# Seams of an MLP: buffers shared across stages, four operands by way of DRAM, another order of products in the down projection

## The chip, the cores and the metric

The kernel runs on one core of one Trainium2 chip. The metric is the device time of one execution in microseconds (us), the median of several runs. Profile times are counted from the start of the span that the profiler recorded.

## What is computed

One layer of a decoder trunk on 2048 rows of 1024 features: a norm, a token mixer (a delta rule group and a dilated attention group of heads), the output projection, and a gated MLP with a causal convolution over the sequence, then a last norm. The end of the layer is what this case is about:

```python
x = x + jnp.concatenate([y_a, y_b], axis=-1) @ w_out[l]
h = rmsnorm(x, ln2[l])
gate = causal_dwconv(h @ w_gate[l], ffn_conv[l])          # three taps, 2816 columns
x = x + (jax.nn.silu(gate) * (h @ w_up[l])) @ w_down[l]
return rmsnorm(x, ln_f)
```

All of it is float32. TensorE takes float32 in a rounded form, so each operand is split into a high and a low part (`split`, L65 to L68: a cast on ACT, then a subtraction on DVE), and each product is three matmuls (`mm3`, L71 to L75): high by high, high by low, low by high.

## The kernel before, in words

The MLP has three stages, each bound to the next by buffers.

**out_proj** (L978) goes through 16 tiles of 128 rows. For each it loads y from DRAM (`wr`, four blocks `yg` of the delta rule and four `ys` of the attention), casts it to yh and yl, and multiplies with w_out, whose eight blocks k are split into woh and wol (`w_out`, L860, two raw buffers `wor`; blocks 0 to 3 are made while the mixer still runs, 4 to 7 at the start of the MLP). The first three tiles (HEAD) run k=0 to 6 first, so that the last head's `ys` may come late. The residual is added on DVE, stored to x1, and normed (`norm2`), and the transposed result goes to DRAM in `hT`.

**gate_up** (L1027) uses Strassen's seven products: rows and features are halved, and for each of 11 pairs of column tiles (p), in each half of the rows (half), there are seven steps s, each of 24 matmuls 128x512 for gate and up (m=0 and 1). One p is 168 matmuls. A step needs one operand of the activations, `hc[s]` (four blocks k, high and low), which serves all 11 p of a half, and one of the weights, wh and wl, which is made two steps ahead (`prep`, AHEAD_W). Of the weights, s=0, 3 and 6 are plain blocks, the others sums made on POOL (sa, sb). `form(half, s)` makes `hc[s]`: s=0, 3, 5 from plain blocks of hT, s=1 and 4 by one subtraction on POOL, s=2 and 6 by one on POOL and one on DVE from an operand that is there already. For half 0 it runs in out_proj (s=0 to 2) and p=0, for half 1 in the last p of half 0 (p=10). `act` does the convolution, silu and product on DVE and ACT; `blocks` makes seven sums of the activation (five on POOL) and stores them in `act`.

**down_proj** (L1163) takes the seven products of the table DOWN, each for eight row groups q: one group is 33 matmuls, whose result is added to or subtracted from acc. Weights `w` are loaded one product ahead; for a sum of two weight blocks POOL adds them (L1183).

The order on each engine and queue is fixed when the program is built; every queue works in order. An instruction that waits holds all that is behind it. Transfers issued by SP also wait for a free slot of its queue.

Of the kernel before, what the change touches and what calls it, by code (L numbers as in the profile page):

```python
# [9 lines left out]
F32 = mybir.dt.float32  # L10
# [8 lines left out]
P = 128  # L19
# [858 lines left out]
def rms_scale(n, ss, src, junk):  # L878
# [12 lines left out]
DOWN = ((((0, 0), 1, (1, 1)), ((0, 0), 1, (1, 1)), ((0, 0, 1), (1, 1, 1))),  # L891
# [7 lines left out]
AHEAD_W = 2  # L899


def phase_e(n):

    with ExitStack() as ctx:
        n.wk = ctx.enter_context(n.pool("ewk"))
        n.lnb = n.wk.tile([P, D], F32, name="lnb")
        n.nc.sync.dma_start(n.lnb, n.a["ln2"].to_broadcast([P, D]))
        with ExitStack() as inner:
            mlp = Mlp(n, inner)
            mlp.out_proj()  # L910
            mlp.gate_up()
        down_proj(n)


class Mlp:
    def __init__(self, n, ctx):
        self.n, self.ctx = n, ctx
        nc = n.nc
        self.sm = ctx.enter_context(n.pool("esm"))
# [11 lines left out]
    def norm2(self, xt, t, tag=None):  # L931
# [3 lines left out]
        ss = n.wk.tile([P, 4], F32, tag="ss", name="ss", bufs=2)  # L935
        rms_scale(n, ss, xt, n.wk.tile([P, D], BF16, tag="junk", name="junk"))
        nc.vector.scalar_tensor_tensor(xt, xt, ss[:, 2:3], n.lnb, op0=ALU.mult, op1=ALU.mult)
# [34 lines left out]

    def out_proj(self):
        n, a = self.n, self.n.a
        nc, tc, v = n.nc, n.tc, n.nc.vector
        with ExitStack() as eo:
# [4 lines left out]
            wp = eo.enter_context(n.pool("ewp", 3))  # L981
            wo = n.wo
# [24 lines left out]
            first = (x for s in range(3) for x in self.form(0, s))  # L1007
            for t in range(HEAD):
                out_proj(t, range(7))
            for t in range(NT):  # L1010
# [5 lines left out]
                xt = xts[t] = n.wk.tile([P, D], F32, tag="xt", name="xt", bufs=3)  # L1016
# [5 lines left out]
                if t >= 11:  # L1022
                    for _ in range(3):
                        next(first, None)
# [3 lines left out]
    def gate_up(self):  # L1028
# [4 lines left out]
        self.hcp += [self.ctx.enter_context(n.pool("ehcb", 1, "right"))] * 4  # L1033
        op = self.ctx.enter_context(n.pool("ego", 1, "right"))
        steps = [(half, p, s) for half in range(2) for p in range(NP) for s in range(7)]
        raws, sums, made = {}, {}, {}

        def load(p, m, blocks):
            w = a["w_gate" if m == 0 else "w_up"]
            for i, j in blocks:  # L1040
                r = raws[m, i, j] = wp.tile([P, 512], F32, tag=f"r{m}{i}{j}", name=f"r{m}{i}{j}")
                nc.sync.dma_start(r, w[2 * p + i][:, 512 * j:512 * j + 512])

        def prep(i):

            half, p, s = steps[i]
            for m in range(2):
# [3 lines left out]
                new = lambda t: wp.tile([P, 512], F32, tag=f"{t}{m}", name=f"{t}{m}")  # L1051
# [65 lines left out]

        for i in range(AHEAD_W):
            prep(i)
# [266 lines left out]
```

## Time and profile before

| | us |
|---|---|
| median of 3 runs | 2922.37 (2922.06 to 2924.52) |
| the profiled execution, its own time | 2918.55 |
| its span | 2916.7 |
| TensorE busy in it | 2752.6 (94%) |
| DVE, ACT, POOL busy | 1669.9, 1131.9, 977.7 |
| mean granted TensorE clock | 0.964 |

Each number in the rows further down is of the one profiled execution. PE is the TensorE, PEld its weight loads, SPq the queue of SyncE that issues DMAs. `A <- B` after a wait names the instruction that ended it. PEclk of 1.00 is the engine's 2.4 GHz, 0.50 its 1.2 GHz. The MLP lies between 1300 and 2917; the mix ends at 1301, out_proj at about 1530, half 0 of gate_up at about 1980, half 1 at 2438.

### The profile page before, as it was taken

The numbers are of one execution on the slowest core, as the hardware profiler recorded it, in microseconds if no ns is written. First come the engines' busy times: TensorE is split into PE (matmuls) and PEld (weight loads), VectorE is DVE, ScalarE is ACT, GpSimd is POOL, SyncE is SP. The second block draws the span as 40 slices with busy tenths as digits, with TensorE's granted clock in tenths as the row PEclk, the third lists the DMA queues.
The fourth block names the chain that finished last, engine by engine and source line by source line (L and its number), as shares of the span: only waits on it lengthen the run. The fifth ranks groups of instructions, "written<-read, shape, count | busy, mean of one in ns | idle before, by whom it ended". The sixth has DMA issues, their size and how long they took to land.

```text
span 2916.7 us, 41147 instructions
## 1 busy us (share of the span) xinstructions
PE 2752.6 (94%) x14974; PEld 2332.3 (80%) x14974; DVE 1669.9 (57%) x2782; ACT 1131.9 (39%) x2349; POOL 977.7 (34%) x1191
## 2 busy tenths in 40 slices
PE   8999999899999999978998999996999996699999
PEld 8998777777899999966776888874888885588887
DVE  5205545725555555533347877778877776445554
ACT  5313554341165555552334333333333332222233
POOL 4200232131122232211116655656655554202231
PEclk9999999999799999988998999998999998899999
DMA  5222344465866665334654333344333325745553
GB/s 182 80 61 98 112 132 136 131 200 167 234 162 166 161 169 142 88 106 144 215 180 145 108 100 106 100 134 152 107 103 97 98 87 187 273 170 175 172 200 132
DMA packets 360665, 416.67 MB, mean 143 GB/s; under 512 B 83287, under 2 KB 249479, under 8 KB 360071
## 3 DMA queue, kind: packets, MB, share of 16 engines
q1 hardware_dynamic: 312848, 384.73, 42.8%
q10 hardware_dynamic: 45390, 20.90, 2.6%
q0 software_dynamic: 2224, 8.42, 1.0%
q8 instruction: 118, 1.93, 0.3%
q14 instruction: 85, 0.70, 0.1%
HBM read 282.16 MB, written 131.79 MB: 142 GB/s over the span
## 4 chain that ended last, share of the span: by engine, by line
PE 82%; DMA 6%; DVE 3%; issue 3%; POOL 3%; ACT 2%; SPq 1%; ACTq 0%; POOLq 0%; DVEq 0%
PE tp L75 7%; PE tp L74 6%; PE tp L73 6%; PE sc L75 6%; PE sc L74 6%; PE sc L73 6%; PE pv L75 5%; PE pv L73 5%; PE pv L74 5%; PE g L73 4%; PE g L75 4%; PE g L74 4%; PE pv L722 3%; PE sc L625 3%; PE sc L627 2%
## 5 line engine op out<-in xcount | busy, mean ns | idle before, releaser
L632 DVE CUSTOM_DVE_ANT_0 s<-sc,bias 128x256 f32<-128x256 f32 (+1 forms) x384 | 121.8, 363 | 130.3 <-PE sc L627 100.6
L1104 POOL TENSOR_TENSOR sm<-cv 128x512 f32<-128x512 f32 x110 | 178.4, 1653 | 52.8 <-issue 26.2
L1183 POOL TENSOR_TENSOR w<-w,w 128x512 f32<-128x512 f32 x55 | 89.1, 1642 | 269.1 <-DMA w<-in_w_down_dram 170.1
L67 ACT CAST ah<-ar 128x1408 fp32r<-128x1408 f32 x56 | 77.1, 1377 | 257.2 <-PE g L74 70.5
L722 PE MATMUL pv<-pt,sv 128*65 128x128 f32 x1200 | 168.0, 285 | 2.3 <-ACT pt L704 2.0
L625 PE MATMUL sc<-k,q 128*128 128x256 f32 (+1 forms) x384 | 156.4, 414 | 1.1 <-DVE m L632 1.0
L67 ACT CAST wh<-r 128x512 fp32r<-128x512 f32 x132 | 81.4, 619 | 192.7 <-issue 59.3
L694 ACT ACTIVATE s<-s,nm 128x256 f32<-128x256 f32 (+1 forms) x384 | 151.5, 460 | 11.7 <-POOL rb L769 6.6
L73 PE MATMUL g<-hch,wh 128*128 128x512 f32 x352 | 141.0, 401 | 14.4 <-DVE g L1143 9.8
L73 PE MATMUL sc<-hch,wh 128*128 128x512 f32 x352 | 140.7, 400 | 12.7 <-ACT hch L67 11.2
L722 PEld LDWEIGHTS pv<-pt,sv 128*65 128x65 f32 x1200 | 143.3, 145 | 5.5 <-ACT pt L704 4.8
L75 PE MATMUL sc<-hch,wl 128*128 128x512 f32 x352 | 140.5, 399 | 5.9 <-DVE wl L68 5.9
L75 PE MATMUL g<-hch,wl 128*128 128x512 f32 x352 | 140.5, 399 | 2.6 <-DVE wl L68 2.6
L68 DVE TENSOR_TENSOR wl<-r,wh 128x512 fp32r<-128x512 f32 x132 | 142.3, 1079 | 0.7 <-ACT wh L67 0.7
L627 PE MATMUL sc<-k,q 128*128 128x256 f32 (+1 forms) x384 | 142.7, 377 | 0.0
L704 ACT COPY pt<-tp 128x512 f32<-128x512 f32 (+1 forms) x152 | 87.7, 578 | 136.1 <-PE tp L701 129.2
L74 PE MATMUL sc<-hcl,wh 128*128 128x512 f32 x352 | 140.2, 398 | 0.0
L74 PE MATMUL g<-hcl,wh 128*128 128x512 f32 x352 | 139.8, 397 | 0.0
L73 PE MATMUL tp<-hch,wh 128*128 128x512 f32 x352 | 138.4, 393 | 0.0
L74 PE MATMUL tp<-hcl,wh 128*128 128x512 f32 x352 | 138.0, 392 | 0.0
L75 PE MATMUL tp<-hch,wl 128*128 128x512 f32 x352 | 138.0, 392 | 0.0
L1084 DVE SCALAR_TENSOR_TENSOR cv<-g,fcw,cv 128x1024 f32<-128x1024 f32 x88 | 132.7, 1508 | 0.8
(373 smaller groups left out, 8228.5 us busy)
## 6 DMA issues: line engine op xcount, KB each, us to landing
ar<-act SPq DMA_DIRECT2D x56, 704.0 KB, 4.2
w<-in_w_down_dram SPq DMA_DIRECT2D x132, 256.0 KB, 5.1
act<-sm SPq DMA_DIRECT2D x110, 256.0 KB, 2.3
r<-in_w_gate_dram SPq DMA_DIRECT2D x88, 256.0 KB, 2.7
r<-in_w_up_dram SPq DMA_DIRECT2D x88, 256.0 KB, 2.9
sm<-hT SPq DMA_DIRECT2D x72, 256.0 KB, 3.5
xt<-in_x_dram SPq DMA_DIRECT2D x32, 512.0 KB, 3.7
zn<-zn SPq DMA_DIRECT2D x32, 512.0 KB, 5.5
```

The costliest lines, as they stand in the source:

```text
L67: (first or nc.scalar.copy)(hi, src)
L68: (e or nc.vector).tensor_tensor(lo, src, hi.bitcast(F32), op=ALU.subtract)
L73: nc.tensor.matmul(ps, ah, bh, start=start, stop=False, skip_group_check=more)
L74: nc.tensor.matmul(ps, ah, bl, start=False, stop=False, skip_group_check=more)
L75: nc.tensor.matmul(ps, al, bh, start=False, stop=stop, skip_group_check=more)
L625: nc.tensor.matmul(r, self.cols(q2, d, u, False, full), self.cols(k1, d, u, prev, full), start=True, stop=False)
L627: nc.tensor.matmul(r, self.cols(q2, d, u, False, full), self.cols(k2, d, u, prev, full), start=False, stop=True)
L632: n.mark = v.tensor_tensor_reduce(out=s[:, r], in0=ps[:, r], in1=self.bias[d][:, bo:bo + r.stop - r.start], scale=1.0, scalar=-3e38, op0=A ...
L694: nc.scalar.activation(s, s, AF.Exp, bias=nm[:, col:col + 1])
L722: nc.tensor.matmul(dst, self.vcols(h, d, u, back), pt[:, j * P:(j + 1) * P], start=(back == int(prev)), stop=(back == 0))
L1084: v.scalar_tensor_tensor(cv, g[:, j:j + 1024], self.cw[:, x, j:j + 1], cv, op0=ALU.mult, op1=ALU.add)
L1104: gp.tensor_tensor(src, x(*op_[0]), x(*op_[2]), op=ALU.add if op_[1] > 0 else ALU.subtract)
```

## The change

Four things are done.

1. The three buffers of y (pool `ewp`) are opened at the very start of the MLP, on other space than before; gate_up then keeps its weights in them: wh and wl of both m lie in one tile of [128, 2, 512], and sa, sb and the raw block (0,1) in the three of `wr`. 
2. `form(0, 3)` moves into out_proj, which begins one tile earlier with this work; p=0 forms s=4, 5, 6 in its steps 0, 1, 2.
3. Of half 1, the operands s=1, 2, 4 and 6 are computed in p=1 to 6 of half 0 (`foresee`, one block at each odd step, 16 in all) and stored in DRAM (`hf`); in p=10 `recall` loads them, two DMAs of 1 MB each. `form(1, s)` is left for s=0, 3 and 5.
4. DOWN begins with a product of one weight block. acc is loaded one tile per group in the first 16 groups, and not all 16 tiles ahead of the second product. The pools of down_proj are opened in another order.

```diff
-DOWN = ((((0, 0), 1, (1, 1)), ((0, 0), 1, (1, 1)), ((0, 0, 1), (1, 1, 1))),
+DOWN = ((((0, 0), 1, (0, 1)), ((1, 1),), ((0, 0, -1), (0, 1, 1))),
+        (((0, 0), 1, (1, 1)), ((0, 0), 1, (1, 1)), ((0, 0, 1), (1, 1, 1))),
...
+EARLY = (1, 2, 4, 6)
...
 class Mlp:
     def __init__(self, n, ctx):
...
+        self.wp = ctx.enter_context(n.pool("ewp", 3))
+        self.wk = ctx.enter_context(n.pool("ewk"))
...
-        self.hcp = [ctx.enter_context(n.pool("ehca"))] * 3
+        self.hcp = [ctx.enter_context(n.pool("ehca"))] * 4
...
+    def foresee(self):
...
+        for k in range(4):
+            for s, first, rest in ((1, (1, 0), ((0, 0),)), (4, (1, 1), ((1, 0),)), (2, (0, 0), ((1, 1), (1, 0))),
+                                   (6, (0, 1), ((0, 0), (1, 1), (1, 0)))):
+                r = load(*first, k)
+                for x in rest:
+                    add = (s == 2 and x == (1, 1)) or (s == 6 and x == (1, 0))
+                    gp.tensor_tensor(r, r, load(*x, k), op=ALU.add if add else ALU.subtract)
+                self.keep(s, k, r)
+                yield
+
+    def keep(self, s, k, src):
+        n = self.n
+        t = self.wk.tile([P, 2, 512], F32R, tag="xt", name="hf", bufs=3)
+        split(n.nc, t[:, 0], t[:, 1], src)
+        n.nc.sync.dma_start(n.hf[s].rearrange("p (i k t) -> p i k t", i=2, k=4)[:, :, k], t.bitcast(F32))
+
+    def recall(self, s):
+        n = self.n
+        self.hc[s] = tuple(self.hcp[s].tile([P, 4, 512], F32R, tag=f"h{i}{s}", name=f"hc{i}{s}") for i in "hl")
+        for i in range(2):
+            t = self.hc[s][i].rearrange("p k t -> p (k t)").bitcast(F32)
+            n.nc.sync.dma_start(t, n.hf[s][:, 2048 * i:2048 * i + 2048])
...
-            wp = eo.enter_context(n.pool("ewp", 3))
-            wo = n.wo
+            wp, wo = self.wp, n.wo
...
-            first = (x for s in range(3) for x in self.form(0, s))
+            first = (x for s in range(4) for x in self.form(0, s))
...
-                if t >= 11:
+                if t >= 10:
...
+        three = [self.wp.tile([P, 2, 512], F32, tag="wr", name="wr") for _ in range(3)]
+        spare = dict(zip(("sa", "sb", "r01"), three))
...
+            lo = self.wp.tile([P, 2, 512], F32R, tag="gul", name="wl")
+            hi = self.wp.tile([P, 2, 512], F32R, tag="guh", name="wh")
...
-                if p == 0 and s < 4:
-                    for _ in self.form(0, s + 3):
+                if p == 0 and s < 3:
+                    for _ in self.form(0, s + 4):
                         pass
                 if p == NP - 1:
-                    for _ in self.form(1, s):
-                        pass
+                    if s in EARLY:
+                        self.recall(s)
+                    else:
+                        for _ in self.form(1, s):
+                            pass
+                elif p and s % 2 == 1:
+                    next(early, None)
...
         prep_a(1)
-        for t in (x for q in range(8) for x in (tile_of(q, 0), tile_of(q, 1))):
+        for t in (x for r in range(2) for q in range(8) for x in (tile_of(7 - q, r),)):
             acc[t] = cp.tile([P, D], F32, name=f"acc{t}")
-            nc.sync.dma_start(acc[t], n.x1[t])
...
+            if x < 16:
+                t = tile_of(q, x // 8)
+                nc.sync.dma_start(acc[t], n.x1[t])
```

How the order of the instructions moves is shown at three places. The first is SP's queue at the end of the mix: rb belongs to the attention, wor is raw w_out, lnb, fcw and xt (from x) are for the later stages, wr is y. Before:

```order
L762 DMA rb<-rden_130 64x512 x2
L907 DMA lnb<-in_ln_dram 128x1024
L924 DMA fcw<-in_fconv_t_dram 128x66
L1017 DMA xt<-in_x_dram 128x1024 x3
L872 DMA wor_12832<-in_w_out_dram 128x1024
L872 DMA wor_12833<-in_w_out_dram 128x1024
L995 DMA wr<-yg_170 128x4x128
L998 DMA wr<-ys_132 128x128
```

After, on the same queue:

```order
L762 DMA rb<-rden_130 64x512 x2
L1029 DMA wr<-yg_174 128x4x128
L1032 DMA wr<-ys_132 128x128
L1032 DMA wr<-ys_133 128x128
L1032 DMA wr<-ys_134 128x128
L1029 DMA wr<-yg_175 128x4x128
L919 DMA lnb<-in_ln_dram 128x1024
L925 DMA fcw<-in_fconv_t_dram 128x66
```

The loads of y have moved ahead of lnb, fcw, x and the last two wor, which now follow the y of all three head tiles.

The second place is p=3 of half 0. On POOL before, from the five sums of an activation (`sm<-cv`) to the weights of the next p (sa, sb; r are raw weights):

```order
L1104 TENSOR_TENSOR sm<-cv 128x512 x5
L1056 TENSOR_TENSOR sa_16139<-r_15986,r_16068 128x512
L1060 TENSOR_TENSOR sb_16184<-sa_16139,r_15984 128x512
L1087 COPY carry<-g_15886 128x2
L1056 TENSOR_TENSOR sa_16145<-r_15990,r_16070 128x512
```

On POOL after (sa and sb are now called wr):

```order
L1144 TENSOR_TENSOR sm<-cv 128x512 x5
L991 TENSOR_TENSOR sm<-sm 128x512 x6
L1127 COPY carry<-g_15877 128x2
L1098 TENSOR_TENSOR wr<-r_15983,r_16074 128x512
L1102 TENSOR_TENSOR wr<-wr,r_15981 128x512
L1098 TENSOR_TENSOR wr<-r_15987,r_16076 128x512
```

On SP after, in the same p, `act` is the store of a sum and r_16074 is the block r011 of the next p, which its sa needs:

```order
L1146 DMA act_0_170<-sm 128x4x128
L982 DMA sm<-hT_154 128x512
L982 DMA sm<-hT_155 128x512 x2
L1146 DMA act_0_172<-sm 128x4x128
L1082 DMA wr<-in_w_gate_dram 128x512
L1082 DMA wr<-in_w_up_dram 128x512
L982 DMA sm<-hT_154 128x512 x2
L999 DMA hf_157<-hf 256x1x512
L982 DMA sm<-hT_155 128x512 x3
L982 DMA sm<-hT_154 128x512
L999 DMA hf_159<-hf 256x1x512
L1082 DMA r_16074<-in_w_gate_dram 128x512
```

Six subtractions of `foresee` have come between the sums and sa on POOL; on SP their loads have come behind the act stores, and two stores of hf ahead of r011.

The third place is SP's queue between gate_up and down_proj. Before:

```order
L1196 DMA ar<-act_0_156 128x1408 x2
L1106 DMA act_1_165<-cv 128x4x128
L1106 DMA act_1_157<-sm 128x4x128
L1106 DMA act_1_161<-sm 128x4x128
L1106 DMA act_1_163<-sm 128x4x128
L1106 DMA act_1_167<-sm 128x4x128
L1106 DMA act_1_169<-sm 128x4x128
L1181 DMA w_21925<-in_w_down_dram 128x512
L1181 DMA w_21927<-in_w_down_dram 128x512
```

After:

```order
L1229 DMA w_21724<-in_w_down_dram 128x512
L1229 DMA w_21729<-in_w_down_dram 128x512
L1146 DMA act_1_165<-cv 128x4x128
L1244 DMA ar<-act_0_160 128x1408 x2
L1229 DMA w_21597<-in_w_down_dram 128x512
L1146 DMA act_1_169<-cv 128x4x128
L1146 DMA act_1_161<-sm 128x4x128
L1146 DMA act_1_163<-sm 128x4x128
```

Thirteen weight loads have moved ahead of the last p's act stores (two of them are shown), and the row of sixteen acc loads, which before followed the 22 weight loads, is spread over the groups.

## Rows read from the trace of the kernel before

**Rows 1.** Windows: us, then busy time (instructions) of each engine, PEclk, DMA share, GB/s.

```profile
1320.00:1360.00 40.00, 33.14 (x133) 26.25 (x134) 7.13 (x10) 5.86 (x9) 0.00 (x0) 0.86 0.33 94
1520.00:1600.00 80.00, 63.30 (x257) 49.88 (x256) 56.52 (x57) 32.75 (x57) 41.23 (x30) 0.89 0.45 148
1600.00:1960.00 360.00, 360.00 (x1562) 292.65 (x1561) 277.38 (x261) 134.84 (x227) 214.74 (x158) 1.00 0.37 110
1960.00:1996.00 36.00, 21.56 (x80) 16.36 (x80) 23.25 (x29) 12.74 (x23) 21.01 (x17) 0.81 0.44 140
1996.00:2032.00 36.00, 22.46 (x78) 16.61 (x76) 34.59 (x28) 16.61 (x29) 25.39 (x18) 0.81 0.49 153
2437.00:2512.00 75.00, 30.44 (x103) 21.47 (x102) 35.82 (x27) 15.68 (x20) 38.51 (x24) 0.68 0.90 328
```

**Rows 2.** Timeline, mix to out_proj: start, us, instruction, [idle before <- what ended it].

```profile
1301.29 0.68 DVE L735 TENSOR_TENSOR acc<-acc,pv 65x512 f32<-65x512 f32 x1 [1.52 <-PE pv L722]
...
1314.86 1.99 ACT L67 CAST woh<-wor 128x1024 fp32r<-128x1024 f32 x2 [14.74 <-DVE rbl L769]
...
1317.24 1.47 SPq L872 DMA_DIRECT2D wor<-in_w_out_dram  x2
1318.80 0.39 SPq L995 DMA_DIRECT2D wr<-yg  x1
...
1326.86 0.80 PE L73 MATMUL g<-woh,yh 128*128 128x512 f32 x1 [25.61 <-ACT yh L67]
```

**Rows 3.** Waits of PE, 1520 to 1600: us in total, times, longest.

```profile
PE g L73 <- DVE g L1143: 8.1, 1, 8.1
PE pv L941 <- DVE xt L937: 5.3, 1, 5.3
```

**Rows 4.** Waits, and then groups of instructions (busy us, mean ns), 1960 to 2035.

```profile
ACT hch L67 <- POOL sm L962: 22.3, 7, 9.9
...
PE sc L73 <- ACT hch L67: 11.2, 1, 11.2
...
L962 POOL TENSOR_TENSOR sm<-sm 128x512 f32<-128x512 f32 x8 | 12.6, 1578 | 12.0 <-DMA sm<-hT 10.8 <-ACT g L1145 1.2
...
L967 DVE TENSOR_TENSOR sm<-sm,hcl 128x512 f32<-128x512 f32 x8 | 9.6, 1207 | 6.2 <-POOL sm L966 6.2
```

**Rows 5.** Timelines of ACT, PE and POOL in one undisturbed p.

```profile
1740.47 1.06 ACT L1088 ACTIVATE cv<-cv 128x1024 f32<-128x1024 f32 x1 [2.78 <-DVE cv L1084]
...
1742.66 0.40 PE L73 MATMUL g<-hch,wh 128*128 128x512 f32 x1
...
1751.79 8.01 POOL L1104 TENSOR_TENSOR sm<-cv 128x512 f32<-128x512 f32 x5 [1.17 <-DVE cv L1089]
...
1756.85 0.58 ACT L1145 COPY g<-g 128x512 f32<-128x512 f32 x1
...
1766.29 1.29 POOL L1056 TENSOR_TENSOR sa<-r,r 128x512 f32<-128x512 f32 x1 [6.49 <-DVE wl L68]
```

**Rows 6.** Groups of POOL and DVE, 1600 to 1960: busy us, mean ns.

```profile
L1066 POOL TENSOR_TENSOR sb<-r,sb 128x512 f32<-128x512 f32 x18 | 40.9, 2271 | 27.5 <-DVE wl L68 27.5
...
L68 DVE TENSOR_TENSOR wl<-r,wh 128x512 fp32r<-128x512 f32 x55 | 59.6, 1083 | 0.0
...
L68 DVE TENSOR_TENSOR wl<-sa,wh 128x512 fp32r<-128x512 f32 x38 | 46.9, 1240 | 1.9 <-ACT wh L67 1.9
```

**Rows 7.** DMA issues on the page: KB each, median us to landing.

```profile
sm<-hT SPq DMA_DIRECT2D x72, 256.0 KB, 3.5
```

**Rows 8.** Timelines of PE, SPq and POOL from 2437, and a wait of PE.

```profile
2442.94 8.91 POOL L1104 TENSOR_TENSOR sm<-cv 128x512 f32<-128x512 f32 x5 [26.23 <-issue]
...
2452.29 16.25 SPq L1181 DMA_DIRECT2D w<-in_w_down_dram  x22
...
2458.59 0.80 PE L73 MATMUL pv<-wh,ah 128*128 128x512 f32 x1 [20.16 <-ACT wh L67]
...
2468.59 15.83 SPq L1241 DMA_DIRECT2D acc<-x  x16
...
PE g L73 <- ACT ah L67: 22.3, 1, 22.3
```

More of the change, by code (lines that the diff above doesn't have):

```diff
@@ L899 @@
 AHEAD_W = 2
+EARLY = (1, 2, 4, 6)
 def phase_e(n):
     with ExitStack() as ctx:
[L905 to L912, printed above, removed]
+        mlp = Mlp(n, ctx)
+        mlp.out_proj()
+        mlp.gate_up()
+    down_proj(n)
 class Mlp:
@@ L918, in __init__ @@
         nc = n.nc
+        self.wp = ctx.enter_context(n.pool("ewp", 3))
+        self.wk = ctx.enter_context(n.pool("ewk"))
+        self.lnb = self.wk.tile([P, D], F32, name="lnb")
+        nc.sync.dma_start(self.lnb, n.a["ln2"].to_broadcast([P, D]))
         self.sm = ctx.enter_context(n.pool("esm"))
@@ L1066, in prep @@
                     gp.tensor_tensor(src, x(0, 1), src, op=ALU.subtract)
[L1067 to L1070 removed]
+                split(nc, hi[:, m], lo[:, m], src)
+                made[i, m] = hi[:, m], lo[:, m]
             if i + 7 < len(steps) and s >= 4:
@@ L1119, in gate_up @@
             prep(i)
+        early = self.foresee()
         for i, (half, p, s) in enumerate(steps):
@@ L1168, in down_proj @@
     with ExitStack() as ctx:
+        wk = ctx.enter_context(n.pool("dwk", 1, "right"))
+        lnb = wk.tile([P, D], F32, name="lnb")
+        cp = ctx.enter_context(n.pool("dcp"))
+        wr = ctx.enter_context(n.pool("dwr"))
         wc = ctx.enter_context(n.pool("dwc"))
         ap = ctx.enter_context(n.pool("dap", 2))
-        wr = ctx.enter_context(n.pool("dwr"))
-        cp = ctx.enter_context(n.pool("dcp", 1, "right"))
         acc, acts, wts, wsum = {}, {}, {}, {}
@@ L1205, in finishing @@
         def finishing(t):
-            ss = n.wk.tile([P, 4], F32, tag="ss", name="ss", bufs=2)
-            o = n.wk.tile([P, D], F32, tag="xt", name="xo", bufs=3)
-            rms_scale(n, ss, acc[t], n.wk.tile([P, D], BF16, tag="junk", name="junk"))
+            ss = wk.tile([P, 4], F32, tag="ss", name="ss", bufs=2)
+            o = wk.tile([P, D], F32, tag="xt", name="xo", bufs=3)
+            rms_scale(n, ss, acc[t], wk.tile([P, D], BF16, tag="junk", name="junk"))
             yield
-            v.scalar_tensor_tensor(o, acc[t], ss[:, 2:3], n.lnb, op0=ALU.mult, op1=ALU.mult)
+            v.scalar_tensor_tensor(o, acc[t], ss[:, 2:3], lnb, op0=ALU.mult, op1=ALU.mult)
             nc.sync.dma_start(n.out[t * P:(t + 1) * P, :], o)
@@ L1301, in trunk @@
     n.hT = [dram.tile([P, KT * 512], F32, name=f"hT{b}") for b in range(NB)]
+    n.hf = {s: dram.tile([P, 4096], F32, name=f"hf{s}") for s in EARLY}
     n.act = [[dram.tile([4 * P, NP * P], F32, name=f"act{i}_{j}") for j in range(2)] for i in range(7)]
```

41 lines of the change are left out of this document (24 added, 17 removed), and 1 row of the table DOWN.

## The prediction

> **What bounds the kernel now.** I read the MLP by stretches first [rows 1]: per stretch the busy time and the number of matmuls (the x behind PE's busy time), because in a stretch with a low granted clock a busy PE does less. In the undisturbed stretch 1600 to 1960 PE does 1562 matmuls in 360 us, one every 0.230 us, at a granted clock of 1.00 and with no idle time at all: there PE is the bound and nothing is to be gained. The other rows are the seams. By count, 1520 to 1600 holds 257 matmuls, 59 us of work in 80; 1960 to 2032 holds 158, 36 us of work in 72; 2437 to 2512 holds 103, 24 us of work in 75. So 21, 36 and 51 us are lost there, and at the first seam a single wait of 25.61 us [rows 2]. Together about 133 us of 2916.7: that is all that a change of seams can touch. Then I read, seam by seam, which wait ends last [rows 2, 3, 4, 8], and for what the change adds, one p of the undisturbed stretch [rows 5].
>
> **Part A, mix to out_proj.** The attention's last pv ends at 1301.3 (the DVE add behind it starts at 1301.29). PE then waits 25.61 us for the first cast of y, at the end of a row on SP's queue: wor for k=6 and 7 at 1317.24, which need the casts of k=4 and 5 (ACT at 1314.86, itself 14.74 late behind the rescale of the last head), and only then y's loads, from 1318.80 [rows 2]. Now y's buffers no longer lie on the attention's, and y's loads stand ahead of lnb, x and those wor. The first y is cast before the last pv ends. PE then has k=0..3 of three tiles, 72 matmuls or about 15.5 us, before it needs the cast of k=4, which is ready at about 1316 (DVE's part at 1317). I count 1 us of wait at the start for the low part of y and 1 to 2 us at k=4. The 25.61 us go, with some 2.5 us of slow clock (1320 to 1360 has a granted clock of 0.86 and 133 matmuls in 33.14 busy us, 0.249 each against 0.230 [rows 1]). Gain 25; bounds 20 (if k=4 to k=7 come late one after the other) and 28.
>
> **Part B, out_proj to gate_up.** 21 us are lost in 1520 to 1600; the two largest single waits are 8.1 us for the accumulate on DVE and 5.3 us for the last norm's xt [rows 3]. The gate weights' first blocks need not wait for out_proj's weights any more, one operand (s=3) is made in out_proj instead of step 0, and the others come a step earlier. Four of seven operands are still formed in p=0, and POOL and DVE stay full there. I take 12; bounds 6 (only the two single waits shrink by half) and 16.
>
> **Part C, half 0 to half 1.** All seven operands of half 1 are formed while PE does p=10 of half 0 and p=0 of half 1: 36 us lost in the 72 from 1960. The waits on PE are one of 11.2 us for hch, and behind it ACT waits 22.3 us for POOL's subtractions, whose mean here is 1.58 us, with DVE's eight further subtractions at 1.21 us each [rows 4]. Now only s=0, 3 and 5 are formed there, each from four plain blocks: 16 casts, 16 low parts, all 16 POOL and 8 DVE subtractions and 24 of 36 loads leave. In their place SP issues eight DMAs of 1 MB. SP holds each pair until PE has done that step, and what is queued behind on SP is the next p's weights, first used five steps later. DVE keeps 12 low parts in p=10 on top of a load that fills three quarters of it [rows 1], so it is nearly full and I leave 4 us lost. Gain 32; bounds 22 and 36. What is late next is the cast of an s=0, 3 or 5 operand ahead of a weight's cast on ACT.
>
> **Part D, gate_up to down.** PE waits 20.16 us for the first weight's cast, and 22.3 us later for ah [rows 8]. The first is the two-block product: 22 weight loads, which SP issues only from 2452.29, behind five act stores, then POOL's sums. The second is the 16 acc loads in one row (15.83 us of SP) ahead of the next weights and the next ar. Now the first product has one block, and nine of its loads are issued in the last p; acc goes one per group over 16 groups. What remains after the last matmul: the last activation, about 5 us (POOL's sums of it start at 2442.94 [rows 8], 4.5 us after PE ends), then 11 low parts on DVE at 1.08 to 1.24 us each beside those sums [rows 6], 12 to 14 us. The first group of 33 matmuls therefore ends some 18 us after gate_up, where 7.6 would do: 10 to 12 us stay lost. Gain 39; bounds 30 (acc, ar and two-block weights together crowd the queue, and one later wait of 9 us stays) and 44.
>
> **The price: operands computed ahead.** During p=1 to 6 of half 0, where PE is the bound, the change adds 28 POOL subtractions, 16 casts, 16 low parts, 44 loads and 16 stores. Against plain idle time this is nothing: POOL waits 6.49 us before sa in each p [rows 5]. But the queues are in order. All subtractions of a p stand on POOL between the five act sums and the next sa; their loads stand on SP behind the act stores; and the load of r011, which sa needs, stands behind one or more of the hf stores. For p=3 (two, three and one subtraction), in us after the p's first matmul, which is at 1742.66 in the undisturbed p of the rows: sums from 9.1; loads out at 15.8 and landed by 20.5 (3.5 each [rows 7]); first item subtracted at 23.1 and stored at 24.6; second item's last loads behind that store, landed at 29, subtracted at 31.6, stored at 33; third subtracted at 34.9; r011 out at 33.4, landed at 36.9; sa, sb, sa at 1.29 each until 40.8; cast 41.4. In before sa was ready at 28. On ACT the first silu stands behind that cast: it was at 36.6 after its p's first matmul (1740.47, a p being 38.76) and comes 4 to 5 us later, so the next p's sums come 4 to 5 us later too, and in that p the first item's cast on ACT stands ahead of the copy of g (at 14.2, needed by PE at 22). The loop closes in 43 us where a p of PE takes 38.76. I get 4 us for p=3, 5 for p=2, where r011 stands behind two stores, 2 to 3 for p=4, none for p=1, 5 and 6 with four or fewer: 12. Bounds: 0, if SP and POOL run further ahead than this; and 40, if every subtraction meets a DVE operation, as L1066 shows at 2.27 us against 1.29 [rows 5, 6] (6 us more per p for six, 3 more for three low parts that wait in turn).
>
> The row on L1066 is a question of who shares a port. The Trainium skill, SBUF — State Buffer, section "Who interferes with whom", says that a DVE instruction with two SBUF inputs and a GpSimd instruction that reads SBUF exclude each other for a whole instruction. The trace agrees: 2.27 against 1.29 us. By that rule taken for every instruction the price is the upper bound, 40; by the idle time of POOL alone it would be 0.
>
> **Sum.** 25 + 12 + 32 + 39 − 12 = 96 us. The profiled execution took 2918.55 (span 2916.7): 2822.5. It lies 3.8 below the median of 2922.37, so on the median's scale 2826. The edits to pools, names and lnb, and the weights' common tile, which makes a cast wait for both halves of the step before (2.8 us later, under the two steps of lookahead), I cost at nothing; if that cover is gone they are part of the 40.
>
> **Rivals.**
> 1. The operands cost nothing. For it: no wait on PE in 360 us, POOL idle. Against it: the queue order above. 2814.
> 2. The first half becomes bound by the shared port and the queues, 40 instead of 12: 2854. For it: 2.27 us rows in every p. Against it: 0.37 DMA share and DVE, POOL at 0.77 and 0.60 busy.
> 3. The late parts give less: at p=10 the 1 MB loads crowd out the weights (8.4 MB of them, 3.1 MB of small loads and 110 GB/s as in 1600 to 1960, some 15 MB in 39 us), and in down acc, ar and w together. Half of C and D is lost, 35: 2861. For it: 16 issues of acc took SP 15.83 us in before [rows 8]. Against it: both have a p or a group of lead.
> 4. Slower than before. The loop of the early operands is hit by transfer times: each of 16 items waits for one more transfer in series. The gain of 108 is eaten when an item costs PE 7 us; this decides when loads there take over 10 us instead of 3.5. Then 16 times 7 to 9 is 112 to 144, and the time 2926 to 2958. Against it: a DMA share of 0.37 [rows 1].
> 5. The change doesn't do what it says: the loads stand early in the order but are held by a queue slot or a buffer. A and D then give nothing but C does: 2890.
>
> **How the numbers follow.** Chances: forecast 0.47 (2812 to 2842), rival 1 0.17, rival 2 0.17, rival 3 0.10, rival 5 0.04, slower 0.04, no change 0.01. The range 2803 to 2866 takes in the forecast, rivals 1 and 2 and most of 3. A measurement of this kernel can tell about 0.2% (6 us) from no change. Faster by more 0.95, within 0.01, slower 0.04.
>
> **What would show it.** A: PE's wait at the mix's end under 3 us, first cast of y before 1302. B: PE idle under 10 us around p=0. C: p=10 of half 0 and p=0 of half 1 together under 85 us (two undisturbed p are 77.5) and no wait on hch above 4. D: first down group ending within 20 us of the last gate_up matmul, no wait of 20. The price: p=3 to 5 of half 0 longer than 38.76 by some us each, the wait being ACT's copy of g or a weight's cast. Wrong if p=1 to 6 take more than 45 us each, or if any single wait of 20 us is left.

## The result, and the profile after

The changed kernel takes 2889.07 us, median of 4 runs (2888.09 to 2890.90), against 2923.44 for the kernel before beside it: ratio 0.988, 95% interval 0.9862 to 0.9897. It is faster by 34 us, where 96 were forecast, and lies above the range's upper end of 2866. The profiled execution took 2890.9 (span 2889.1), 27.65 less than the profiled one before; the stages below are measured on that pair.

The same stretches as in [rows 1], windows of the kernel after (us, then busy time and instructions of PE, PEld, DVE, ACT, POOL, then PEclk, DMA share, GB/s):

```profile
1320.00:1360.00 40.00, 38.22 (x171) 30.30 (x170) 18.92 (x22) 14.19 (x21) 7.63 (x10) 1.00 0.67 200
1520.00:1600.00 80.00, 76.42 (x324) 60.78 (x324) 63.25 (x65) 31.76 (x55) 49.63 (x35) 0.99 0.47 145
1600.00:1960.00 360.00, 321.28 (x1309) 253.83 (x1308) 258.95 (x235) 116.14 (x203) 231.31 (x160) 0.95 0.45 137
1960.00:1996.00 36.00, 36.00 (x155) 28.89 (x155) 32.93 (x30) 14.82 (x26) 21.17 (x15) 1.00 0.49 158
1996.00:2032.00 36.00, 29.71 (x117) 23.23 (x116) 27.12 (x29) 15.67 (x27) 22.06 (x12) 0.91 0.64 252
2437.00:2512.00 75.00, 65.77 (x266) 52.42 (x265) 47.48 (x45) 21.45 (x26) 27.24 (x16) 0.91 0.71 259
```

Every stretch in which matmuls were missing has more of them: 171 for 133, 324 for 257, 272 for 158, 266 for 103. The stretch that was full has fewer: 1309 in 1600 to 1960, where 1562 were done in [rows 1]. At 0.230 us each that is 58 us lost in the one place where TensorE had had no idle time.

The first cast of y and the first matmul of out_proj, timeline of the kernel after (start, us, instruction):

```profile
1302.66 0.94 ACT L67 CAST yh<-wr 128x896 fp32r<-128x896 f32 x1
...
1303.66 0.50 PE L73 MATMUL g<-woh,yh 128*128 128x512 f32 x1
```

No wait stands before that matmul, where 25.61 us stood in [rows 2]. And the start of down, again from the timeline of the kernel after:

```profile
2447.38 0.39 PE L75 MATMUL sc<-hch,wl 128*128 128x512 f32 x1
2453.25 0.79 PE L73 MATMUL pv<-wh,ah 128*128 128x512 f32 x1 [5.48 <-ACT ah L67]
```

5.48 us for 20.16, and the 22.3 us for ah behind it [rows 8] are gone. What came in their place, waits of PE in the kernel after, 1573 to 1868 (us in total, times, longest):

```profile
PE g L73 <- ACT g L1186: 24.2, 8, 5.2
PE sc L73 <- ACT u L1186: 15.6, 3, 7.7
```

By stages. A runs from the last matmul of the mix to the last of out_proj, B from there to s=3 of p=1, C is p=10 and the p=0 behind it, D runs from the last matmul of gate_up to the last of down (a p is counted from its step s=3 to that of the next p):

| | gain forecast | gain measured |
|---|---|---|
| mixer, whose code is the same | 0 | −2.7 |
| A, mix to out_proj | 25 | 22.3 |
| B, out_proj to gate_up | 12 | 11.2 |
| C, half 0 to half 1 | 32 | 26.8 |
| D, gate_up to down | 39 | 37.4 |
| operands computed ahead, p=1 to 6 of half 0 | −12 | −59 |
| every other p: 39.2 instead of 38.76 us | 0 | −8 |

The six p of half 0 took 47.3, 51.2, 48.4, 51.6, 46.1 and 49.7 us, 294.3 in all; six undisturbed ones of the same kernel take 235.2. Two steps of the working failed, the price and one that it did not contain.

One of these p in the kernel after, rows of POOL, SP's queue, ACT and PE; p=3 begins at 1650.7, its s=3 at 1671.7:

```profile
1676.18 1.30 POOL L1144 TENSOR_TENSOR sm<-cv 128x512 f32<-128x512 f32 x1 [2.60 <-DMA act<-sm]
1678.82 2.60 POOL L991 TENSOR_TENSOR sm<-sm 128x512 f32<-128x512 f32 x2 [1.34 <-DMA sm<-hT]
1685.35 1.28 POOL L991 TENSOR_TENSOR sm<-sm 128x512 f32<-128x512 f32 x1 [3.93 <-DMA sm<-hT]
...
1674.06 1.44 SPq L982 DMA_DIRECT2D sm<-hT  x3
...
1681.45 0.62 ACT L67 CAST hf<-sm 128x512 fp32r<-128x512 f32 x1 [13.52 <-POOL sm L991]
1681.98 0.58 ACT L1186 COPY g<-g 128x512 f32<-128x512 f32 x1
...
1682.61 0.79 PE L73 MATMUL g<-hch,wh 128*128 128x512 f32 x1 [5.16 <-ACT g L1186]
1683.20 0.63 PE L74 MATMUL g<-hcl,wh 128*128 128x512 f32 x1
```

ACT stands idle for 13.52 us before the cast of an operand that is needed only in half 1, and the copy of g, for which TensorE waits at once, stands behind it. The next matmuls start 0.43 us apart, in place of 0.23, some seven times: the granted clock is at its lower level (1.2 GHz) behind the wait, 0.51 in the mean from 1682.6 to 1686.1. So a p pays twice, as the window from s=3 of p=2 to that of p=3 shows:

```profile
1620.40:1671.70 51.30, 42.84 (x170) 33.51 (x169) 33.73 (x32) 14.75 (x26) 32.64 (x23) 0.90 0.49 149
```

51.30 − 42.84 = 8.5 us of idle time, and 42.84 − 39.2 = 3.6 us in which PE is busy at a mean clock of 0.90.

### The profile page after: what moved, and what is told of

It is laid out like the page before. It is cut to its first block, busy times and chain, and to the rows that moved or that the text cites. A ratio compares the mean times of both kernels' runs of the same rounds, so it can differ in the third digit from the quotient of the medians.

```text
span 2889.1 us, 41075 instructions
## 1 busy us (share of the span) xinstructions
PE 2777.6 (96%) x14974; PEld 2344.6 (81%) x14974; DVE 1676.2 (58%) x2774; ACT 1122.1 (39%) x2349; POOL 1036.1 (36%) x1203
## 4 chain that ended last, share of the span: by engine, by line
PE 38%; DMA 5%; POOL 4%; DVE 4%; issue 2%; SPq 1%; ACT 1%; POOLq 0%; DVEq 0%; ACTq 0%
PE tp L75 4%; PE tp L73 4%; PE tp L74 4%; PE sc L75 3%; PE sc L73 3%; PE sc L74 3%; PE g L75 3%; PE g L74 3%; PE g L73 3%; DMA sm<-hT 3%; PE pv L74 3%; PE pv L75 3%; PE pv L73 3%; POOL sm L1144 2%; DVE wl L68 1%
## 5 line engine op out<-in xcount | busy, mean ns | idle before, releaser
L68 DVE TENSOR_TENSOR wl<-wr,wh 128x512 fp32r<-128x512 f32 x220 | 270.4, 1259 | 38.3 <-ACT wh L67 37.4
L67 ACT CAST wh<-wr 128x512 fp32r<-128x512 f32 x220 | 135.7, 623 | 180.2 <-POOL wr L1102 54.5
L632 DVE CUSTOM_DVE_ANT_0 s<-sc,bias 128x256 f32<-128x256 f32 (+1 forms) x384 | 121.8, 363 | 124.6 <-PE sc L627 97.6
L73 PE MATMUL sc<-hch,wh 128*128 128x512 f32 x352 | 142.1, 404 | 16.4 <-ACT u L1186 15.6
L1124 DVE SCALAR_TENSOR_TENSOR cv<-g,fcw,cv 128x1024 f32<-128x1024 f32 x88 | 126.0, 1432 | 1.5
```

Source lines behind the costliest of these rows:

```text
L67: (first or nc.scalar.copy)(hi, src)
L68: (e or nc.vector).tensor_tensor(lo, src, hi.bitcast(F32), op=ALU.subtract)
L73: nc.tensor.matmul(ps, ah, bh, start=start, stop=False, skip_group_check=more)
L632: n.mark = v.tensor_tensor_reduce(out=s[:, r], in0=ps[:, r], in1=self.bias[d][:, bo:bo + r.stop - r.start], scale=1.0, scalar=-3e38, op0=A ...
L1124: v.scalar_tensor_tensor(cv, g[:, j:j + 1024], self.cw[:, x, j:j + 1], cv, op0=ALU.mult, op1=ALU.add)
```

## The experiments

Executions differ: in the profiled runs the mixer, the same code in all, ends between 1298 and 1316. So beside the medians stands the time from the mixer's end to the last matmul of down (MLP: 1608.2 before, 1577.5 after), and "lost" is what the p's of half 0 with early operands take above an undisturbed p of the same run. Both are read from the one profiled execution of each run. The medians of e2, e8, e9, e15 and e16 are single executions.

| run | what | median | MLP | lost |
|---|---|---|---|---|
| after | | 2889.07 | 1577.5 | 59 |
| e1 | nothing computed ahead | 2864.71 | 1547.7 | 0 |
| e2 | ahead, without loads | 2857.84 | 1548.7 | 29 |
| e15 | ahead, without subtractions | 2879.89 | 1557.5 | 37 |
| e5 | cast a step later | 2883.30 | 1569.8 | 50 |
| e6 | two items a p, p=1 to 8 | 2889.31 | 1576.8 | 52 |
| e10 | e6, casts tied behind copies | 2872.27 | 1558.4 | 37 |
| e13 | loads together, subtractions behind the weights' sums | 2873.94 | 1560.5 | 37 |
| e11 | e10, addresses | 2863.39 | 1551.3 | 46 |
| e14 | e13, addresses | 2862.03 | 1546.8 | 47 |
| e16 | e13 without subtractions | 2841.49 | 1527.1 | 3 |
| e17 | e13, only s=1 and 4 ahead, addresses | 2842.50 | 1529.1 | 10 |
| e12, e18 | e1, addresses | 2843.68, 2847.09 | 1530.1, 1530.3 | 0 |

### Is the loss that of the early operands at all?

Theory: the 59 us are theirs. Rival: the shared buffers of the weights slow half 0. e1 forms all operands of half 1 in p=10:

```diff
-EARLY = (1, 2, 4, 6)
+EARLY = ()
...
-                elif p and s % 2 == 1:
-                    next(early, None)
```

> The changed kernel without the operands computed ahead: all seven operands of half 1 are formed from p=10 on, as before the change; all else of the change stays. Theory (the 16 items of foresee cost PE about 59 us in p=1 to 7 of half 0 and give back some 27 us at the seam between the halves): the periods of p=1 to 7 fall from 46 to 52 us to 39.2, the seam loses 27 to 33 us again, the time is 2857 to 2863 us. Rival (the long periods come from the weights' common buffers or from the moved loads, not from foresee): the periods stay at 46 us or more and the time is above 2900.

Measured 2864.71, ratio 0.9775 (0.9751 to 0.9799), just above the expectation; the rival falls. Every p of p=1 to 9 takes 39.2 us. At the seam to half 1, p=10 and p=0 take 115.5 us together, as before the change (114.2); in the changed kernel they take 87.4. So computing ahead gave back 28 us at the seam and cost 59: without it the change brings 66 us by that ratio, and not 34.

### Loads or subtractions?

e2 takes the 44 loads away (the subtractions read operands that are there); e15 takes the 28 subtractions away and leaves all else. In both, and in e16, half 1's numbers are others.

```diff
-                r = load(*first, k)
+                r = self.small()
+                src = self.hc[0][0][:, k].bitcast(F32)
...
-                    gp.tensor_tensor(r, r, load(*x, k), op=ALU.add if add else ALU.subtract)
+                    gp.tensor_tensor(r, src, self.hc[3][0][:, k].bitcast(F32), op=ALU.add if add else ALU.subtract)
+                    src = r
```

> The changed kernel, where foresee keeps its 28 POOL subtractions, 16 casts, 16 DVE low parts and 16 stores, but takes its inputs from operands that lie in SBUF in place of the 44 loads from DRAM, which are left out (so half 1 is computed from other numbers). Theory (a loop of in-order queues in which POOL waits for loads that wait for buffers, ACT waits for POOL, and PE waits for ACT's copy): without the loads the periods of p=1 to 7 fall to 39 to 42 us, the time is 2830 to 2845 us. Rival (DVE and POOL exclude each other at the shared port, as the row of 2.27 us shows): all the port work is still there, the periods stay at 46 to 50 us, the time is 2880 to 2890 us.

29 of the 59 us remain, between the two expectations. The casts still stand ahead of the copy; timeline of e2, ACT and PE:

```profile
1668.02 1.14 ACT L67 CAST hf<-sm 128x512 fp32r<-128x512 f32 x2 [5.38 <-POOL sm L986]
1669.06 0.58 ACT L1182 COPY g<-g 128x512 f32<-128x512 f32 x1
...
1669.69 0.79 PE L73 MATMUL g<-hch,wh 128*128 128x512 f32 x1 [5.91 <-ACT g L1182]
```

```diff
...
-                    gp.tensor_tensor(r, r, load(*x, k), op=ALU.add if add else ALU.subtract)
+                    load(*x, k)
```

> The changed kernel with the operands computed ahead as before, but without the 28 GpSimd subtractions: all 44 loads of hT, 16 casts, 16 low parts and 16 stores stay; the items stored are the first block alone, so half 1's numbers differ. The changed kernel loses 59 us in p=1 to 6. Theory (a cast of hf stands ahead of a copy that TensorE needs, and waits for whatever makes its item; the subtraction is the last and longest link): without the subtractions the cast waits for one load only, and at most 20 of the 59 us remain: p=1 to 6 of 39 to 43 us, time 2840 to 2855. Rival (the loads' round trip and the stores ahead of them make the item late, whatever is computed): the loss stays at 35 us or more, p's of 45 us and more, time above 2862.

37 remain, as the rival said, in p's of 44 to 48 us. Without any arithmetic the cast waits for a load instead; waits of ACT in e15, 1560 to 1860, and of PE, 1583 to 1857:

```profile
ACT hf L67 <- DMA sm<-hT: 78.6, 13, 10.1
...
PE g L73 <- ACT g L1185: 23.3, 10, 3.1
```

So neither part is the cause alone; with either of them left, the cast is late enough to hold the copy.

### Another place for the cast

e5 puts the cast and the store one step behind the subtractions; e6 also spreads the items, two a p (the second condition below is e5's; in e6 it is `s > 2`).

```diff
+                yield
                 self.keep(s, k, r)
...
-                elif p and s % 2 == 1:
+                elif p and s:
```

> The changed kernel, where the cast, the low part and the store of each block computed ahead are written one step after its subtractions (three items a p in p=1 to 6, as before; loads unchanged). Theory (the loss has two parts: ACT's cast, which waits for POOL's subtraction ahead of the copy of g, on which PE waits; and the serial loads, which delay POOL's sa and with it the next p's sums): the first part goes, the loads and the 4 to 6 subtractions of a p stay, periods of 41 to 46 us, time 2845 to 2870 us. Rival (the loads alone make the loop): periods stay at 46 to 52 us, 2889 us.

> The same late cast, and two items a p in p=1 to 8, subtracted at s=3 and 5 and cast at s=4 and 6, when the sums of the activation are done and their buffers are free. Theory (order and buffers make the loss, not the amount of work): nearly nothing is left of it, periods of 39.2 to 41 us in p=1 to 8, the time is 2830 to 2848 us. Rival (the port is full: 28 subtractions and 16 low parts, some 47 us at their undisturbed price, don't fit beside the rest whatever their place): 35 us or more of the 59 remain, 2865 us or more.

Both theories miss: 2883.30 and 2889.31, where at most 2870 and 2848 were expected. e6 came out where its rival said (35 us or more remain; 52 do), but for another reason than the amount of work: the order in which the program is written does not settle the order on ACT. In e6 the cast stands ahead of the copy of u (timeline, ACT):

```profile
1677.74 0.62 ACT L67 CAST hf<-sm 128x512 fp32r<-128x512 f32 x1 [15.43 <-POOL sm L991]
1678.27 0.61 ACT L67 CAST wh<-wr 128x512 fp32r<-128x512 f32 x1
1678.79 0.58 ACT L1187 COPY u<-sc 128x512 f32<-128x512 f32 x1
```

e10 is e6 with the order tied: each cast behind the copy of u, each low part behind the DVE add.

```diff
+        n.tc.add_manual_dep(hi.ins, self.copied.ins.name, info, reason="cast behind copy")
+        n.tc.add_manual_dep(lo.ins, self.added.ins.name, info, reason="low part behind add")
```

> As in the run with two items a p (28 subtractions, 44 loads, 16 casts, 16 low parts and 16 stores all kept), but each cast is tied behind ACT's copy of u of step s=2, and each low part behind DVE's add of the step before, so that no copy on which PE waits stands behind them; the stores of hf thereby come behind the load of r011. Theory (the loss is where the cast stands on an in-order engine): periods of 39.2 to 41 us in p=1 to 9, the time is 2835 to 2848 us. Rival (the amount of work at the shared port): periods of 43 us or more, 2870 us or more.

2872.27, ratio 0.982 (0.9791 to 0.9848), just inside what the rival said; 37 us remain. The copies are no longer behind the casts. What the cast holds instead is the next thing on ACT and DVE; waits of e10, 1613 to 1790, then of PE, 1520 to 2200:

```profile
ACT hf L999 <- POOL sm L991: 68.1, 6, 15.6
POOL sm L991 <- DMA sm<-hT: 29.9, 6, 7.1
...
PE g L73 <- DVE g L1189: 18.6, 4, 4.9
```

e13 takes the loop out: all loads of two items go out together, the subtractions stand on POOL behind the weights' sums, so that the loads have landed when they begin, and the casts behind the copy.

```diff
+                    sub = gp.tensor_tensor(r, r, t, op=ALU.add if add else ALU.subtract)
+                    n.tc.add_manual_dep(sub.ins, self.sb.ins.name, info, reason="behind sb")
```

> The changed kernel with the same 28 subtractions, 44 loads, 16 casts, 16 low parts and 16 stores of the operands computed ahead, two items a p in p=1 to 8, but: all loads of a p's two items go out together a step after the activation's sums (the spare halves of lnb and the four small buffers hold them), POOL subtracts them behind sa and sb of the next p, and ACT and DVE cast them three steps later, behind the copy of u of s=2. Theory (the loop sums, act stores, loads, subtractions, sa, silu, sums of in-order queues makes the loss): that loop no longer holds the items, periods of 39.2 to 40.5 us in p=1 to 9, the time is 2828 to 2840 us. Rival (the work is too much for the port DVE and POOL share): the periods stay at 42 us or more, 2860 us or more.

2873.94 (ratio 0.9842, 0.9819 to 0.9865), as the rival said: 37 us remain again, though ACT's longest wait before such a cast is 4.7 us, where it was 15.6 in e10. e16 is e13 without the subtractions, all else kept.

> The order with the items' loads together and their casts behind the copy (37 us lost over p=2 to 8), without its 28 GpSimd subtractions; loads, casts, low parts and stores stay. Theory (what is left there is VectorE slowed by GpSimd at the shared port: the same product cv<-cv,u takes 2.32 us there against 1.57 before): p=1 to 8 come within 1 us of the undisturbed 39.2, in all at most 8 us of the 37 remain, and cv<-cv,u is back under 1.8 us. Rival (loads, stores and casts in the queues): 20 us or more remain.

Here the theory holds: 3 us remain. The same DVE product `cv<-cv,u` and the subtractions in e13 (one line's durations, min, median and max in ns, with first and last start):

```profile
L1146 DVE TENSOR_TENSOR cv<-cv,u x8: 2296/2318/2334, 1653.4 to 1795.2; 128x1024 f32<-128x1024 f32 x8
...
L1000 POOL TENSOR_TENSOR lnb<-lnb,sm x14: 1732/1772/2295, 1652.9 to 1789.7; 128x512 f32<-128x512 f32 x14
```

and in e16:

```profile
L1142 DVE TENSOR_TENSOR cv<-cv,u x8: 1210/1211/1212, 1640.6 to 1768.6; 128x1024 f32<-128x1024 f32 x8
```

With subtractions on POOL beside it each of the eight products takes 2.32 us, without them 1.21; the subtractions take 1.77 instead of 1.3. VectorE's taps, with products and low parts between them, lead to silu, and the copy of g stands behind silu on ACT: the chain comes late, the copy with it, and PE waits as in the changed kernel (18.6 us for ACT's g in e13, 2.3 in e16, over the same p's). The Trainium skill, SBUF — State Buffer, section "Who interferes with whom", says that a DVE instruction with two SBUF inputs and a GpSimd instruction that reads SBUF contend for one read interface; these rows agree.

How the delay reaches PE shows in one p of e13 (timeline, DVE and ACT):

```profile
1696.60 2.33 DVE L1146 TENSOR_TENSOR cv<-cv,u 128x1024 f32<-128x1024 f32 x1
...
1705.79 1.06 ACT L1145 ACTIVATE cv<-cv 128x1024 f32<-128x1024 f32 x1 [7.43 <-DVE cv L1141]
1706.76 0.57 ACT L1203 COPY g<-g 128x512 f32<-128x512 f32 x1
```

From the p's first product to this silu VectorE works without a gap. In p=2 to 8 that takes 9.1 to 9.2 us in e13 and 7.0 in e16. The silu is 3.6 us later in e13 in the mean, counted from the p's s=3: 2.2 of them are this stretch, 1.4 its later start, and how much of those 1.4 is the subtractions' own time on POOL, no run tells.

In the changed kernel the port is not what holds PE. There the same stretch takes 7.0 to 7.2 us in p=1 to 6, as in the undisturbed p's behind them (7.2), and the 28 subtractions take 1.29 us in the median; the products (p=2 to 6, as above):

```profile
L1129 DVE TENSOR_TENSOR cv<-cv,u x10: 1209/1211/2317, 1655.8 to 1858.6; 128x1024 f32<-128x1024 f32 x10
```

(A single product of 2.31 us stands in undisturbed p's of e1 too.) What is late there is the start of the stretch: 31 to 36 us behind the p's s=3, and 21 in an undisturbed p. So the port is the price that stays once the order is mended, as in e13, and what the rows of the changed kernel show is the order of the queues and the round trips of hT.

e17 keeps 8 of the 28 subtractions in that order: only s=1 and s=4 are computed ahead, with the addresses of the next section. e18 is its measure, e12 again.

```diff
-EARLY = (1, 2, 4, 6)
+EARLY = (1, 4)
...
-        for k, group in ((k, g) for k in range(4) for g in ((6, 1), (2, 4))):
+        for k, group in ((k, g) for k in range(4) for g in ((4, 1),)):
```

> Only the operands of s=1 and s=4, which take one subtraction each, are computed ahead (8 subtractions, 8 items, 16 loads), in the order with the loads together, the subtractions behind the weights' sums and the casts behind the copy, and with the three pads; s=2 and s=6 are formed at the seam from the others, as before. Theory (the price is proportional to the work at the shared port, 34 us for 28 subtractions): 10 us over p=1 to 6, and 12 to 18 back at the seam, where 40 are lost without anything ahead: 2834 to 2842, a little under the kernel with nothing computed ahead and the same pads. Rival (the seam is bound by s=2 and s=6, which stay): no gain at the seam, 2848 or more.

> Nothing computed ahead and three pads, the same program as e12 again, as the measure for e17 on the same chip: 2838 to 2850.

The price is 9.7 us for 8 subtractions with their loads and casts, 1.2 each; in e13 against e16 it is 34 for 28, again 1.2 each. The seam gains 10.6 (p=10 and p=0 take 106.2 us, 116.8 in e12), less than the 12 to 18 expected. So the balance is nil: 2842.50 (ratio 0.9725, 0.970 to 0.975) and 2847.09 (0.9744, 0.9719 to 0.9769) can't be told apart.

### The 0.44 us in every undisturbed p

A p takes 39.2 us after and 38.76 before, with no wait in either. Windows 2080 to 2380, of before:

```profile
2080.00:2380.00 300.00, 300.00 (x1303) 243.99 (x1302) 231.23 (x216) 112.61 (x189) 173.58 (x117) 1.00 0.34 103
```

of after:

```profile
2080.00:2380.00 300.00, 300.00 (x1288) 240.98 (x1287) 239.24 (x217) 107.14 (x183) 181.50 (x116) 1.00 0.33 100
```

and of e12 below:

```profile
2080.00:2380.00 300.00, 300.00 (x1326) 248.47 (x1325) 252.51 (x222) 110.64 (x190) 187.09 (x118) 1.00 0.34 103
```

PE is busy throughout at a clock of 1.00 in all three and does 1303, 1288 and 1326 matmuls of one shape. By steps: before has matmuls 226.7 ns apart at s=0 to 2 and 233.3 at s=3 to 6, after 233.3 at all seven. The change moved the tiles: in the compiled programs the address of the weights less that of the operand is, modulo 256 bytes, 0 at s=0 to 2 and 224 at the others before, 224 everywhere after. The theory in e3 was that equal addresses modulo 64 are enough; a pad moves the tiles.

```diff
+        keep.tile([P, 8], F32, name="pad")
...
+        op.tile([P, 8], F32, name="pad")
```

> The changed kernel with two pads of 32 bytes per partition, which move the seven operands of gate_up to an address that is a multiple of 64, as the weights' is. Theory (a matmul whose two operands differ by 32 in their address modulo 64 takes 233.3 ns per 512 columns and not 226.7): all matmuls of gate_up go at 226.7, the undisturbed period falls from 39.2 to 38.1 us, 16 periods that PE bounds give 18 us, the time is 2864 to 2871 us. Rival (the spacing depends on the side of SBUF, the pool or the traffic, not on the address): 39.2 us as before, 2889 us.

> The kernel before the change, with one pad of 32 bytes that moves the operands s=3 to 6 to a multiple of 64 (s=0 to 2 lie on one already). Theory of the address: the steps s=3 to 6 fall from 233.3 to 226.7 ns per matmul, the undisturbed period from 38.76 to 38.1 us, 19 such periods give 13 us, the time is 2908 to 2911 us. Rival (pool or side): no change, 2923 us.

e4 (one such pad in the kernel before) came out as expected: 2908.86, ratio 0.9944 (0.9925 to 0.9963), all steps 226.7. e3 missed: 2889.35, four steps at 228.9, three at 226.7, and half 0's early p's no shorter. There the difference was 192 and 0. e7 (e6 with pads) has 128 at s=0 to 3, with 233.3, and 0 at s=4 to 6, with 226.7; a difference of 160 is that of out_proj in the changed kernel, at 233:

> The kernel of the run with two items a p, with pads of 96, 32 and 96 bytes, so that the seven operands and the weights of gate_up, and y and w_out of out_proj, all lie on multiples of 128. Theory of the address (226.7 ns where both operands of a matmul have the same address modulo 128, 229 where they differ by 64, 233.3 where by 32): gate_up's 3696 matmuls gain 6.6 ns each where PE is the bound, 24 us, and out_proj's 768 some 5 us: 24 to 30 us faster than the run without pads. Rival (only a multiple of 64 counts): 18 to 22 us.

It gained 5 us (2884.68) and not 24 to 30, since those four steps were as slow as before. Modulo 256 fits all of these, and foretold e11 (e10 with other pads), e12 (e1 with them) and e14 (e13 with them), where every step is at 226.7:

```diff
+        op.tile([P, 24], F32, name="pad")
...
+        keep.tile([P, 56], F32, name="pad")
...
+        op.tile([P, 8], F32, name="pad")
```

> The ordered kernel with pads of 224, 32 and 96 bytes, by which the moving operand and the weights of every matmul of gate_up and out_proj have the same address modulo 256. The runs so far have 226.7 ns where the two addresses differ by 0 modulo 256, 228.9 where by 192, and 233.3 where by 128, 160 or 224. Theory (the difference modulo 256 counts): all seven steps at 226.7, a period of 38.1 us, out_proj too: 25 to 30 us less than the ordered kernel, 2806 to 2820 us. Rival (the place of the first four operands, not their address): s=0 to 3 stay at 229 to 233 ns, 12 to 18 us less.

> The kernel without operands computed ahead, with the same pads of 224, 32 and 96 bytes. By the address theory 25 to 30 us less than without the pads, 2835 to 2841 us; by the rival 12 to 18 us less. Beside the ordered kernel with pads it tells what the operands by way of DRAM are worth once they cost PE nothing: 20 to 28 us.

> The same with the pads of 224, 32 and 96 bytes. By the address theory all periods fall by 1.1 us where PE bounds them, out_proj by 5 us: 24 to 30 us less, 2800 to 2815 us, and 25 to 40 us faster than the padded kernel without operands computed ahead (2843.68). Rival (shared port): no faster than that kernel.

e12 is at 2843.68 (ratio 0.9728, 0.969 to 0.9765), 21 us under e1 by the medians and 17.6 by the MLP, less than the 25 to 30 expected: the p's gained their 1.1 us each, but p=10 and p=0 together took 1.3 us more than in e1 and out_proj gained 1.3 us and not 5. e11 (2863.39) and e14 (2862.03) gained 9 and 12 only: an undisturbed p fell by 1.1 us, the p's with early operands did not (46 us lost in e11, 47 in e14). PE waits in each of them, and a faster PE only waits longer.

### Down's two parts

e8 restores the order of products and loads acc two a group; e9 restores the 16 acc loads in one row.

```diff
...
-            if x < 16:
-                t = tile_of(q, x // 8)
-                nc.sync.dma_start(acc[t], n.x1[t])
+            if x < 8:
+                for t in (tile_of(q, 0), tile_of(q, 1)):
+                    nc.sync.dma_start(acc[t], n.x1[t])
```

> The changed kernel with the old order of products in down (a sum of two weight blocks first); acc is then needed for both rows of a group at once, so two acc loads go with each of the first 8 groups. Theory (the first product's weight sums on POOL, behind the activation's five sums, held the first weight back): from the last gate_up matmul to the end 15 to 25 us more than the 433.7 us of the changed kernel. Rival (the early loads alone gave the gain): under 5 us more.

> The changed kernel, where all 16 acc loads are issued in one row ahead of the first group, as before the change; the one-block product stays first. Theory (the row of 8 MB holds back the next weights and the next ar): 10 to 20 us more from the last gate_up matmul to the end than the 433.7 us of the changed kernel. Rival (with the first product's weights already there the row is hidden): under 3 us more.

From the last matmul of gate_up to the last of down: 433.7 us after, 439.5 in e8 (2899.18), 455.2 in e9 (2917.03). So the row of acc loads is worth 21.5 us, a little over the theory, and the order of products, with acc spread in either case, 6, where the theory said 15 to 25. In e9 the row is back on SP's queue (timeline):

```profile
2467.62 11.52 SPq L1290 DMA_DIRECT2D acc<-x  x13
```

and with it the wait for ah (waits of PE in e9 from 2440):

```profile
PE g L73 <- ACT ah L67: 16.5, 1, 16.5
```

## Why the prediction was wrong, step by step

- **What bounds the kernel**: right. The 133 us in the seams were what could be had, and 97.6 of them came.
- **A, 25**: 22.3. The wait of 25.61 is gone, as worked out, but out_proj itself took 200.8 us instead of 197.2. The first y is cast at 1302.66, not before 1302, but the mixer too ended 2.7 us later. The waits of 1.8 us for woh and 0.8 for yl are those named.
- **B, 12**: 11.2. p=0 takes 39.2 instead of 48.5, and PE is idle 3.6 us in 1520 to 1600.
- **C, 32**: 26.8. No wait on hch is left, as said; one of 6.3 us for a weight's low part on DVE remains, where 4 us in all were left for. p=10 and p=0 took 87.4 us together instead of under 85.
- **D, 39**: 37.4. The first group began 5.5 us behind gate_up and ended 21.1 us behind it, where 18 were worked out and 20 were the mark. Of the two causes named, the row of acc loads is worth 21.5 us (e9) and the order of products 6 (e8); the other 10 were not tried apart.
- **The price, 12**: 59. This is the step that failed. The mechanism in the text is the one in the rows: an early operand's cast ahead of the copy of g, held by round trips of hT. Two things were mis-sized. First, only p=3, 2 and 4 were charged, since the others have four or fewer subtractions; but it is the first item that holds the copy, and every p has one. p=1, 5 and 6 lost 8, 7 and 10 us, and all six took more than 45, the mark for being wrong. Second, the first item of p=3 came later than worked out. Counted from s=3, which the undisturbed p reaches 16.3 us behind its first matmul, it was put at 6.8 us against a need of the copy at 5.7. PE wanted the copy at 5.8, but the cast ran at 9.8, since a sum waited 2.60 us for its buffer and the loads went out at 2.4 and not at −0.5. A slip of a few us was counted once per loop, and not as a wait of PE in each p with the lower clock behind it (8.5 and 3.6 us in p=2).
- **The bound of 40** was the port alone, and left the order out. The subtractions come to 34 us in e13's order (e13 against e16), within it. But the changed kernel's 59 are of another kind: its products and subtractions run at 1.21 and 1.29 us in the median, as if undisturbed, and in e10 and e13 tying the order took 22 us off.
- **Costed at nothing**: the pools. No wait came of them, but new addresses did: 0.44 us in each of the 22 p, some 10 us. No row of the trace before says so in words; that s=0 to 2 ran at 226.7 ns and s=3 to 6 at 233.3 stood there unread.
- **Rivals**: 2, the port and the queues, was right in the queues, at too low a price. Rival 4 (each item waits for one more transfer in series) has the right chain too, but 59 us over 16 items are 3.7 us an item, half of what would have made the kernel slower, and the loads of hT took 4.2 us in the median of the page, not over 10. Rival 5's number, 2890, is the measured one by chance: by it A and D give nothing, and they gave 22.3 and 37.4.

What stays open: how the 59 us divide among loads, subtractions and order can't be said exactly. Taking out the loads or the subtractions, or tying the order, brings 30, 22 and 22 us, more together than there is, because they hide one another. Only with the order tied and the subtractions gone (e16) is the loss gone, but for 3 us.

## What to carry to other kernels

Before work is put beside a bound engine, ask of each of its instructions not whether its engine is idle but what stands behind it in that engine's queue and when that is needed; an idle engine with a due copy behind a waiting cast costs the bound engine all of the wait that lies behind the copy's due time, and the clock after it. Where the order is mended and VectorE's chain leads to the bound engine, price added GpSimd work at about its own duration: in e13 and e17 1.2 us for each subtraction, so that 28 of them could not pay for a seam of 28 us. And when a change moves buffers, compare the spacing of the bound instruction before and after, step by step, where nothing waits.

## What the runs showed of the hardware

The spacing of float32 matmuls of 128x512 follows the addresses of their two operands: 226.7 ns where the weights and the moving operand have the same address modulo 256 bytes, 228.9 at a difference of 192, 233.3 at 128, 160 and 224, in all the stages looked at (out_proj goes from 233 to 227 in e7, e11 and e12; down is at 226.7 in all). In gate_up's 3696 matmuls the 6.7 ns come to 24.6 us. The differences not listed weren't tried, and why it is so no run shows.

Behind the wait of 5.16 us some seven matmuls ran at the lower clock, about 0.2 us longer each, 1.5 us; over the window of p=2, with waits of 6.0 and 2.4 us, it was 3.6. A row of PE's waits therefore tells less than what the waits cost.
